# Opening with an fp32 spread of c's first row, and weight casts ordered behind a latent norm's squares

## The chip, the cores and the metric

The kernel runs on one core of one Trainium2 chip. A core has five engines with a queue each: PE (TensorE, the matmuls), DVE (VectorE), ACT (ScalarE), POOL (GpSimd) and SP (SyncE, which here only starts DMAs). Each executes its own list of instructions in order; semaphores make one list wait for another. The metric is the device time of one execution in microseconds (us).

## The reference

A two-layer hybrid transformer on 256 latent tokens and 256 context tokens of width 1024. Layer 0 mixes with grouped-query attention, layer 1 with a bidirectional mLSTM; each layer has a half feed-forward before and after its mixer, and everything is modulated by vectors made from `c` (latent) and `c_ctx` (context). Only the latent tokens come out. Cut to what the change touches:

```python
def half_ffn(h, shift, scale, gate, w_in, w_out, g, b):
    xm = modulate(h, shift, scale)
    a, u = jnp.split(xm @ w_in, 2, axis=-1)
    y = (jax.nn.silu(a) * u) @ w_out
    return post_norm(h, 0.5 * gate * y, g, b)          # layer norm of ALPHA*h + delta

for i in range(DEPTH):
    mod_lat = jnp.split((silu(c) @ ada_w[i] + ada_b[i])[:, None, :], N_MOD, axis=-1)
    mod_ctx = jnp.split((silu(c_ctx) @ ada_w[i] + ada_b[i])[None, None, :], N_MOD, axis=-1)
    h_lat = half_ffn(h_lat, mod_lat[0], mod_lat[1], mod_lat[2], ...)
    h_ctx = half_ffn(h_ctx, mod_ctx[0], mod_ctx[1], mod_ctx[2], ...)
    ...                                                 # mixer, post_norm, second half_ffn
return h_lat
```

## The kernel before

**Layout and precision.** Activations lie transposed: `h[:, d, t]` holds feature block d (eight blocks of 128) for 512 tokens, latents first. A product of full fp32 accuracy is made from three one-pass matmuls (`mm3`, L230, L233, L234): a tensor x is split into a rounded part `xh` and the rest `xl`, a weight chunk into `wh` and `wl`, and wh·xh + wh·xl + wl·xh is summed in PSUM. Plain fp32 matmuls, which the hardware makes in several passes, are left for small things.

**Weights.** A chunk of 128 x 1024 fp32 (512 KB) comes by DMA into a ring of `RAW = 4` buffers. `split` (L213 on ACT, L218 on DVE) makes `wh` by a cast on ACT and `wl` by subtractions on DVE, in four pieces of 256 columns in the feed-forwards, into a ring of `WB = 7` pairs. So a raw buffer is free for the next DMA only after the chunk's last low piece on DVE. Each of `split`'s instructions goes through `behind`: where `self.fence` names an instruction of the same engine, the new one is ordered behind it. This edge has no semaphore; it only constrains the order in which the scheduler writes out each engine's list at build time.

**The norms.** `norm` (n0 to n4, one behind each half feed-forward or mixer but the last) is a generator that `steps` advances between matmuls. For one group (latents `LAT` or context `CTX`) it does: the mean by a matmul with a constant (L425, as all its matmuls); per feature block d, z = h − mean on DVE (L447) and its square on ACT (L454); sums of the squares on DVE (L464) and POOL; the variance by 128x1 matmuls (L425); 1/sqrt in small steps (L483 to L486 and L271 to L275); a diagonal matrix of it on DVE (L490), spread over the partitions by another L425 matmul (`rb`); per block x, `xh`, `xl` (L520 on DVE, L521 on ACT, L522 on DVE), which the next weights' matmuls need. The latent norm comes first, the context norm some 10 to 20 us behind it. PE fills the waits with products of the weights that come next: rows of these products are placed between the norm's matmuls by the scheduler. n4 has a latent norm only and is "raw": `xh` and `xl` are made from z before the variance is known (L451, L452), so the first three units of the last feed-forward multiply un-normed data and are corrected behind it; their matmuls are 258 columns wide.

**The opening.** `start` makes the first modulation vectors itself. The 16 values of silu(c) per partition (`b.ct`, one set for the latents, v = 0, one for the context, v = 1) are spread by `replicate(v)` into rows that are equal on all partitions (`b.cb`), for dot products on DVE (`by_dve`). `by_pe(d)` makes the modulation of block d by 128x2 fp32 matmuls instead. `products(d)` then are the first feed-forward's matmuls, 512 columns wide. `b.ct` is split into `parts` (L1557, L1547), and `unit` is a copy of the identity in the one-pass type (L1556). All of it is pinned: its order is the order in which it is written.

Of the kernel before, what the change touches and what calls it, by code (L numbers as in the profile page):

```python
# [13 lines left out]
AF = mybir.ActivationFunctionType  # L14
# [4 lines left out]
P = 128  # L19
D = 1024  # L20
ND = D // P
# [138 lines left out]
class Body:  # L160
# [24 lines left out]
    def mm(self):  # L185
        return self.t([P, 512], tag="mm", bufs=6, pool=self.pp)
# [217 lines left out]
    def pin(self, ins):  # L404

        return self.tc.keep_in_program_order(ins)
# [14 lines left out]
    def norm(self, g, coef, keep=True, nxt=True, alone=False, log=False):  # L421


        nc, V, S = self.nc, self.nc.vector, self.nc.scalar
        mm = lambda *k, **kw: self.pin(nc.tensor.matmul(*k, **kw))  # L425
# [6 lines left out]
        v = 0 if t0 == 0 else 1  # L432
        most = g == LAT
# [10 lines left out]
        for d in range(ND):  # L444
            yield
            z = self.h[:, d, t0:t1]
            V.tensor_tensor(out=z, in0=z, in1=m[:, :w], op=ALU.subtract)  # L447
            if raw:
                c = coef()[1][:, v, d : d + 1]
                xh = self.xh[:, d, TL:T]  # L450
                S.activation(xh, z, AF.Copy, scale=c)  # L451
                V.scalar_tensor_tensor(self.xl[:, d, TL:T], z, c, xh.bitcast(F32), ALU.mult, ALU.subtract)  # L452
            q = self.tmp(w)
            S.activation(q, z, AF.Square)  # L454
            if d in (SQA if alone else SQPE):
                sums[d] = q, q
                continue
            eng = nc.gpsimd if d in (POOLA if alone else POOLD) else V
            if eng not in sums:
                sums[eng] = q, None  # L460
            else:
                a, s2 = sums[eng]
                s2 = s2 or self.t([P, TL], tag="s1", bufs=S1B)
                eng.tensor_tensor(out=s2, in0=a, in1=q, op=ALU.add)  # L464
                sums[eng] = s2, s2
# [10 lines left out]
        pin = self.pin  # L476
        if most:
# [3 lines left out]
            for i in range(n):  # L481
                c = var[:, n + i : n + i + 1]
# [11 lines left out]
        if most:  # L494
# [3 lines left out]
            for d in range(ND):  # L498
                if eng[d] is not V:
                    z = self.h[:, d, t0:t1]  # L500
# [10 lines left out]
        for d in range(ND):  # L511
            yield
            z = self.h[:, d, t0:t1]
            if most and eng[d] is V:
                V.tensor_tensor(out=z, in0=z, in1=dls, op=ALU.subtract)
            ab, c, e = coef()
# [57 lines left out]
    def ffn(self, layer, s, gate, groups, side, start=None):  # L574
# [7 lines left out]
        with self.tc.tile_pool(name=f"ffn{li}", bufs=1) as gp:  # L582
# [3 lines left out]
            if start:  # L586
                start(self)
                done = NSTART
# [892 lines left out]
def start(b):  # L1481

    nc, pin = b.nc, b.pin
    V, S = nc.vector, nc.scalar
    mm = lambda *k, **kw: pin(nc.tensor.matmul(*k, **kw))  # L1487
    dma = lambda *k: pin(nc.sync.dma_start(*k))
    rep = [[b.mm() for _ in range(2)] for _ in range(2)]
    acc = [b.mm() for _ in range(6)] + [b.ps()]  # L1490
    dots = b.ps()
    c0, e0, mod = b.modv(), b.modv(), b.t([P, 2, 2, ND])
    raws, ws = {}, {}

    def load_dots(d, chs=(1, 0)):
        if d not in raws:
            raws[d] = b.pair(F32)
        for ch in chs:
            dma(raws[d][ch], b.a["ada_p"][PEDOT.index((ch, d))] if (ch, d) in PEDOT else b.a["ada_w"][0, ch * ND + d])

    def load(d):
        dma(b.h[:, d, :], b.a["xt"][:, d, :])
        r = b.t([P, 1024], tag="raw", bufs=RAW)[:, : 7 * P]
        dma(r, b.a["start_in"][d][:, : 7 * P])
        ws[d] = [r] + b.pair(n=7 * P)
        pin(S.copy(ws[d][1], ws[d][0]))

    def bias(ch, d):
        return b.b1[:, d : d + 1] if ch else b.vec[:, V_ADAB + d : V_ADAB + d + 1]

    def replicate(v):
        for k in range(ND):
            for i, c in enumerate(parts):
                mm(rep[v][k // 4][:, k % 4 * P : (k % 4 + 1) * P], c[:, k, v : v + 1].broadcast_to([P, P]), unit, start=i == 0, stop=i == 1)
        for i in range(2):
            pin(V.tensor_copy(b.cb[:, v, i * 512 : (i + 1) * 512], rep[v][i]))

    def by_pe(d):
        o = {ch: dots[:, 4 * d + 2 * ch : 4 * d + 2 * ch + 2] for ch in (1, 0) if (ch, d) in PEDOT}
        for ch in o:  # L1520
            for k in range(ND):
                mm(o[ch], raws[d][ch][:, k * P : (k + 1) * P], b.ct[:, k, :], start=k == 0, stop=k == ND - 1)
        for ch in o:
            pin(S.activation((e0, c0)[ch][:, :, d], o[ch], AF.Identity, bias=bias(ch, d)))

    def by_dve(d):
        for ch in (0, 1):
            if (ch, d) not in PEDOT:
                for v in range(2):
                    to = mod[:, ch, v, d : d + 1]  # L1530
                    pin(V.scalar_tensor_tensor(b.tmp().bitcast(BF16), raws[d][ch], 1.0, b.cb[:, v, :], ALU.mult, ALU.mult, accum_out=to))
                pin(V.tensor_scalar((e0, c0)[ch][:, :, d], mod[:, ch, :, d], bias(ch, d), None, ALU.add))
                yield

    def modulated(d):
        xs = []
        for v, g in enumerate((LAT, CTX)):
            xs.append((b.xl[:, d, g[0] : g[1]], b.tmp(TL), b.xh[:, d, g[0] : g[1]]))
            b.later.append((b.h[:, d, g[0] : g[1]], ALPHA, None, None))
        for o in (2, 1):  # L1540
            for v, g in enumerate((LAT, CTX)):
                last = pin(S.activation(xs[v][o], b.h[:, d, g[0] : g[1]], AF.Identity, bias=e0[:, v, d : d + 1], scale=c0[:, v, d : d + 1]))
        b.fence = {last.ins.engine: last} if d == ND - 1 else {}
        return xs

    def low(l, x, h):
        return pin(V.tensor_tensor(out=l, in0=x, in1=h.bitcast(F32), op=ALU.subtract))  # L1547

    def products(d):
        for i, (w, x) in enumerate(((1, 0), (2, 0), (1, 1))):  # L1550
            for n, o in enumerate(acc):
                mm(o, ws[d][w][:, n * P : (n + 1) * P], b.x(d, BOTH)[x], start=not d and not i, stop=d == ND - 1 and i == 2)

    parts = [b.tmp(2 * ND).bitcast(F32R).rearrange("p (n f) -> p n f", f=2) for _ in range(2)]
    unit = b.tmp(P).bitcast(F32R)
    pin(V.tensor_copy(unit, b.ident))  # L1556
    pin(S.copy(parts[0], b.ct))  # L1557
    low(parts[1], b.ct, parts[0])
    replicate(0)
    load_dots(0)  # L1560
    load(0)
    replicate(1)
    low(ws[0][2], ws[0][0], ws[0][1])
    by_pe(0)
    load_dots(1)
    xs = {0: modulated(0)}
    for d in range(ND):
        n = d + 1
        rows = by_dve(n) if n < ND else iter(())
        if n < ND:  # L1570
            load(n)
        if n + 1 < ND:
            load_dots(n + 1)
        next(rows, None)
        for x in xs[d]:
            last = low(*x)
        for _ in rows:
            pass
        if n < ND:
            low(ws[n][2], ws[n][0], ws[n][1])  # L1580
            by_pe(n)
            xs[n] = modulated(n)
        products(d)
    b.fence[last.ins.engine] = last
    for j in range(NSTART - 1):
        b.ffn_g(j, acc[2 * j], acc[2 * j + 1], BOTH)
    r, (h, l) = b.t([P, 1024], tag="raw", bufs=RAW), b.pair()
    nc.sync.dma_start(r.rearrange("p (d f) -> p d f", d=ND), b.a["start_in"].rearrange("d p f -> p d f")[:, :, 7 * P :])
    b.split(r, h, l)
    o = b.mm()  # L1590
    for k in range(ND):
        c = slice(k * P, (k + 1) * P)
        b.mm3(o, (h[:, c], l[:, c]), b.x(k, BOTH), k == 0, k == ND - 1)
    b.ffn_g(NSTART - 1, acc[6], o, BOTH)


def emit(ctx, tc, a, out):
# [56 lines left out]
    both = (LAT, CTX)  # L1654
    feeds = [feed(q, dots, 0 if i else ROOM[0][1]) for i, (q, dots) in enumerate(zip(queue, DOTS))]
    norm("n0", lambda: b.ln_mod(0, 0, (0, 3)))
    b.ffn(0, 0, once("g0", lambda: b.half_gate(0, 2)), both, feeds[0], start)
    feeds[0].done()
    cpool.close()
    norm("n1", lambda: b.ln_mod(0, 1, (0, 6)), log={LAT: "kept", CTX: "kept"})  # L1660
    b.attention(lambda: b.shift_(0, 5))
    cpool = b.silu_c()
    b.pending = [lambda: b.silu_load(lambda ins: b.after(ins, b.silu) if ins.ins.engine == b.silu.ins.engine else ins)]
    norm("n2", lambda: b.ln_mod(0, 2, (1, 0)))
    b.ffn(0, 1, once("g1", lambda: b.half_gate(0, 8)), both, feeds[1])
    feeds[1].done()
# [106 lines left out]
```

## Time and profile before

| | us |
|---|---|
| median of three runs (lowest, highest) | 1653.3 (1652.46, 1655.67) |
| the profiled execution: its own time | 1652.55 |
| its span (first to last instruction) | 1650.6 |
| PE busy in it | 1617.8 (98%) |
| DVE busy | 1407.3 (85%) |
| ACT busy | 752.0 (46%) |
| POOL busy | 161.2 (10%) |

PE is busy nearly throughout, so the time is PE's work plus the few places where it waits. The largest of these waits is at the very start (6.36 us), the others, below 2.1 us each, are mostly in the norms. Busy shares of the other engines are averages: in a norm DVE is busy without a break. A matmul record is longer than its share of the pipeline (0.28 us for one of 256 columns that starts 0.12 us after the one before), so the work of a stretch is read from counts and starts, not from record lengths.

### The profile page before, as it was taken

To read this page: it belongs to the slowest core of one execution; us is meant where nothing else is said; L and a number is where in the kernel's file an instruction comes from. 1 tells how busy PE (TensorE), PEld (TensorE's weight loads), DVE (VectorE), ACT (ScalarE), POOL (GpSimd) and SP (SyncE) were. 2 spreads that over 40 slices of the span, in tenths; PEclk is the share of its full clock that TensorE was granted. 3 is DMA by queue.
4 is the path that set the end of the run, shared out by engine and by line. 5 is a ranking of instruction groups with operands and counts; after the bars stand their busy time and mean duration, and the time that the engine had idled before them with its cause. 6 is when DMAs were issued, how large, how long until landed. Compare 5 with 4: busy or idle time off the path is not lost. (4 is left out here: it accounts for less than half of the span.)

```text
span 1650.6 us, 27339 instructions
## 1 busy us (share of the span) xinstructions
PE 1617.8 (98%) x10496; PEld 1472.2 (89%) x10496; DVE 1407.3 (85%) x2859; ACT 752.0 (46%) x1370; POOL 161.2 (10%) x237
## 2 busy tenths in 40 slices
PE   8999999999999999999999999999999999999998
PEld 7888888889988998899899998998999978999986
DVE  5999999979888998888797899898797968997686
ACT  4632223315666364255354453453453646566542
POOL 0011111102231210000000200000001002120000
PEclk9999999999999999999999999999999999999999
DMA  6777777742202544435334444335232342437552
GB/s 257 269 255 253 228 248 240 233 153 87 65 1 63 182 151 142 153 123 162 111 116 141 179 153 141 115 111 184 90 121 98 96 141 77 134 105 260 180 179 75
DMA packets 72210, 250.65 MB, mean 152 GB/s; under 512 B 7952, under 2 KB 11024, under 8 KB 72080
## 3 DMA queue, kind: packets, MB, share of 16 engines
q1 hardware_dynamic: 53360, 182.93, 33.7%
q0 software_dynamic: 17856, 65.02, 12.3%
q8 instruction: 82, 1.34, 0.3%
q10 hardware_dynamic: 864, 0.96, 0.2%
q14 instruction: 48, 0.39, 0.1%
HBM read 247.83 MB, written 1.05 MB: 151 GB/s over the span
## 5 line engine op out<-in xcount | busy, mean ns | idle before, releaser
L233 PE MATMUL t<-t,t 128*128 128x256 f32 (+2 forms) x2072 | 676.2, 327 | 1.2 <-DVE t L522 0.8
L230 PE MATMUL t<-t,t 128*128 128x256 f32 (+2 forms) x2072 | 675.3, 328 | 1.8 <-ACT t L213 1.7
L234 PE MATMUL t<-t,t 128*128 128x256 f32 (+2 forms) x2072 | 673.3, 326 | 1.4 <-DVE t L218 1.4
L213 ACT CAST t<-t 128x1024 fp32r<-128x1024 f32 (+3 forms) x390 | 329.2, 866 | 308.9 <-PE t L234 145.7
L218 DVE TENSOR_TENSOR t<-t,t 128x256 fp32r<-128x256 f32 (+2 forms) x726 | 415.6, 613 | 50.0 <-ACT t L213 48.3
L233 PEld LDWEIGHTS t<-t,t 128*128 128x128 f32 x2072 | 391.2, 189 | 37.1 <-DVE t L522 1.5
L230 PEld LDWEIGHTS t<-t,t 128*128 128x128 f32 x2072 | 388.6, 189 | 38.3 <-ACT t L213 3.2
L234 PEld LDWEIGHTS t<-t,t 128*128 128x128 f32 x2072 | 389.6, 188 | 35.8 <-DVE t L218 1.6
L825 PEld LDWEIGHTS t<-t,t 128*128 128x128 f32 x2436 | 288.9, 189 | 3.2 <-ACT t L833 1.5
L825 PE MATMUL t<-t,t 128*128 128x256 f32 x2436 | 289.9, 281 | 1.4 <-ACT t L833 0.9
L338 DVE SCALAR_TENSOR_TENSOR t<-t,t 128x1024 bf16<-128x1024 f32 x224 | 265.8, 1218 | 1.6 <-DMA t<-in_ada_w 1.5
L760 ACT CAST t<-t 128x512 fp32r<-128x512 f32 (+1 forms) x116 | 108.7, 941 | 148.9 <-DVE t L762 103.7
L330 POOL DMA_DIRECT2D t<-in_ada_w x124 | 66.5, 536 | 798.2 <-DVE t L338 733.7
L761 DVE TENSOR_TENSOR t<-t,t 128x512 fp32r<-128x512 f32 (+1 forms) x116 | 125.3, 1086 | 6.8 <-ACT t L760 6.2
L624 DVE SCALAR_TENSOR_TENSOR t<-t,t,t 128x256 f32<-128x256 f32 x128 | 56.6, 477 | 49.6 <-PE t L234 49.6
L1033 PE MATMUL t<-t,t 128*128 128x256 f32 (+1 forms) x256 | 78.7, 308 | 1.0 <-DVE t L218 1.0
L1032 PE MATMUL t<-t,t 128*128 128x256 f32 (+1 forms) x256 | 79.2, 310 | 0.0
L1034 PE MATMUL t<-t,t 128*128 128x256 f32 (+1 forms) x256 | 78.7, 309 | 0.0
L568 ACT ACTIVATE t<-t 128x256 f32<-128x256 f32 (+1 forms) x64 | 30.1, 479 | 103.3 <-PE t L234 100.9
L1487 PE MATMUL t<-t,t 128*128 128x512 f32 (+2 forms) x280 | 61.1, 378 | 6.9 <-DVE t L1547 6.4
L1487 PEld LDWEIGHTS t<-t,t 128*128 128x128 f32 x280 | 53.5, 234 | 14.0 <-issue 6.3
L967 PE MATMUL t<-t,t 128*128 128x512 f32 x264 | 60.0, 389 | 0.0
(200 smaller groups left out, 1481.5 us busy)
## 6 DMA issues: line engine op xcount, KB each, us to landing
t<-in_ffn_in SPq DMA_DIRECT2D x168, 512.0 KB, 4.5
t<-in_ada_w POOLq DMA_DIRECT2D x124, 512.0 KB, 4.1
t<-in_ffn_out SPq DMA_DIRECT2D x68, 512.0 KB, 4.5
t<-in_ffn_last SPq DMA_DIRECT2D x22, 512.0 KB, 3.5
t<-in_ada_w SPq DMA_DIRECT2D x15, 512.0 KB, 8.5
t<-in_att_in SPq DMA_DIRECT2D x12, 512.0 KB, 3.8
t<-in_att_out SPq DMA_DIRECT2D x8, 512.0 KB, 3.6
t<-in_ml_qk SPq DMA_DIRECT2D x8, 512.0 KB, 3.6
```

Source lines behind the costliest of these rows:

```text
L213: self.behind(self.nc.scalar.copy(h, x))
L218: self.behind(self.nc.vector.tensor_tensor(out=ls, in0=xs, in1=hs.bitcast(F32), op=ALU.subtract))
L230: ins = mm(out, wh, xh, start=first, stop=False)
L233: mm(out, wh, xl, start=False, stop=False)
L234: mm(out, wl, xh, start=False, stop=last)
L338: ins = nc.vector.scalar_tensor_tensor(self.tmp().bitcast(BF16), r, 1.0, self.cb[:, v, :], ALU.mult, ALU.mult, accum_out=to)
L760: high = lambda p, r: pin(S.copy(p[0], r))
L761: low = lambda p, r: pin(V.tensor_tensor(out=p[1], in0=r, in1=p[0].bitcast(F32), op=ALU.subtract))
L825: pin(nc.tensor.matmul(o, p, q, start=first and k == i == 0, stop=k == half - 1 and i == 2, skip_group_check=True))
L1032: mm(o, self.xh[:, k, c], wh, start=k == 0, stop=False)
L1033: mm(o, self.xh[:, k, c], wl, start=False, stop=False)
L1487: mm = lambda *k, **kw: pin(nc.tensor.matmul(*k, **kw))
```

## The change

Two edits that do not touch each other.

```diff
@@ norm
-            S.activation(q, z, AF.Square)
+            square = S.activation(q, z, AF.Square)
+            if most and d == ND - 1:
+                self.fence = {square.ins.engine: square}
@@ start
-    def replicate(v):
+    def replicate(v, parts, unit):
         for k in range(ND):
             for i, c in enumerate(parts):
-                mm(rep[v][k // 4][...], c[:, k, v : v + 1].broadcast_to([P, P]), unit, start=i == 0, stop=i == 1)
+                mm(rep[v][k // 4][...], c[:, k, v : v + 1].broadcast_to([P, P]), unit, start=i == 0, stop=i == len(parts) - 1)
@@ start, the order
+    replicate(0, [b.ct], b.ident)
     parts = [...]
     unit = b.tmp(P).bitcast(F32R)
-    pin(V.tensor_copy(unit, b.ident))
     pin(S.copy(parts[0], b.ct))
     low(parts[1], b.ct, parts[0])
-    replicate(0)
+    pin(V.tensor_copy(unit, b.ident))
     load_dots(0)
     load(0)
-    replicate(1)
+    by_pe(0)
     low(ws[0][2], ws[0][0], ws[0][1])
-    by_pe(0)
+    replicate(1, parts, unit)
```

The opening: row v = 0 is spread by eight fp32 matmuls of `b.ct` itself with the identity, which need neither `parts` nor `unit`; row v = 1 still by sixteen one-pass matmuls, but behind `by_pe(0)`. The fence: in each latent norm (`most` is true for the latents), the square of the last block becomes ACT's fence, so every cast that `split` emits later in the program (weights, and the gated products of the feed-forward) is ordered behind it.

Lines 455 to 1519 of before are 2 higher in the change, later ones 5 higher; the names of the tiles that stand for one weight chunk are 8 lower. Three places of the engines' lists:

PE, the opening, before. `t_101` and `t_102` are the two `parts`, `t_103` is `unit`; `t_86` to `t_89` are the four halves of the two spread rows, `t_97` the dots of `by_pe(0)` (16 matmuls) and `by_pe(1)` (8), `t_90` the first product. The last two one-pass matmuls of the spread and what follows:

```order
L1487 MATMUL t_89<-t_103,t_101 128x128
L1487 MATMUL t_89<-t_103,t_102 128x128
L1487 MATMUL t_97<-t_72,t_125 128x2 x16
L1487 MATMUL t_97<-t_72,t_170 128x2 x8
L1487 MATMUL t_90<-t_68,t_131 128x512
```

And PE's first rows of the change (`t_72` is `b.ct`, `t_70` the identity):

```order
L1489 MATMUL t_86<-t_70,t_72 128x128 x4
L1489 MATMUL t_87<-t_70,t_72 128x128 x4
L1489 MATMUL t_97<-t_72,t_117 128x2 x16
L1489 MATMUL t_88<-t_113,t_111 128x128
L1489 MATMUL t_88<-t_113,t_112 128x128
```

32 one-pass matmuls ahead of `by_pe(0)` became 8 fp32 ones; 16 one-pass ones stand behind it now, ahead of `by_pe(1)`. Nothing else changes in PE's list up to the products.

PE, norm n1 (behind the attention), at the variance of its context norm (L425 into `t_5767`), before. The first chunks of the next feed-forward are `t_5711`, `t_5743`, `t_5800`, `t_5832`, `t_5873`:

```order
L234 MATMUL t_5869<-t_68,t_5873 128x256
L230 MATMUL t_5870<-t_68,t_5873 128x256
L233 MATMUL t_5870<-t_69,t_5873 128x256
L234 MATMUL t_5870<-t_68,t_5873 128x256
L230 MATMUL t_5869<-t_68,t_5873 128x256
L425 MATMUL t_5767<-t_61,t_5673 128x1
```

In the change the same place (the chunks are `t_5703`, `t_5735`, `t_5792`, `t_5824`, `t_5865` now, the variance `t_5759`):

```order
L230 MATMUL t_5699<-t_68,t_5735 128x256
L233 MATMUL t_5699<-t_69,t_5735 128x256
L230 MATMUL t_5700<-t_68,t_5735 128x256
L233 MATMUL t_5700<-t_69,t_5735 128x256
L234 MATMUL t_5699<-t_68,t_5735 128x256
L234 MATMUL t_5700<-t_68,t_5735 128x256
L425 MATMUL t_5759<-t_61,t_5665 128x1
```

Before, the 96 matmuls of the first four chunks and 13 of the fifth stand between PE's first use of the first chunk and this variance; in the change the 48 of the first two chunks and 8 others do. The 53 others stand behind the variance and ahead of the context's `rb` (82 matmuls between the two now, 29 before); from there on the two lists have the same rows again. On ACT the casts of the first four chunks moved behind the eight squares of n1's latent norm (three of them stood ahead of all squares, one between the sixth and the seventh), on DVE their low pieces accordingly.

ACT, norm n4, before: `t_15502` to `t_15705` are the first six chunks of the last feed-forward (two to a unit), `t_15395` the last chunk of the mixer's output; then the norm's blocks begin (`t_68` is `xh`):

```order
L213 CAST t_15395<-t_15393 128x1024
L213 CAST t_15502<-t_15500 128x1024
L213 CAST t_15534<-t_15532 128x1024
L213 CAST t_15601<-t_15599 128x1024
L213 CAST t_15633<-t_15631 128x1024
L213 CAST t_15673<-t_15671 128x1024
L213 CAST t_15705<-t_15703 128x1024
L451 ACTIVATE t_68<-t_67,t_15415 128x256
L454 ACTIVATE t_15432<-t_67 128x256
```

And in the change, from the last block's pair on:

```order
L451 ACTIVATE t_68<-t_67,t_15407 128x256
L454 ACTIVATE t_15482<-t_67 128x256
L213 CAST t_15494<-t_15492 128x1024
L213 CAST t_15526<-t_15524 128x1024
L213 CAST t_15593<-t_15591 128x1024
L213 CAST t_15625<-t_15623 128x1024
L213 CAST t_15665<-t_15663 128x1024
L213 CAST t_15697<-t_15695 128x1024
```

All six casts went from ahead of the sixteen block instructions to behind them, and two more casts that stood further on follow directly (before, one of these was between the sixth and seventh block). On DVE 22 of their low pieces went from ahead of the norm's blocks to between the blocks and the variance's L483, so that 23 pieces stand there. PE's list still has the 48 matmuls of the first two chunks ahead of the variance (54 of the first three before), and 14 matmuls of the mixer's last output between the mean and those.

In n0, n2 and n3 the shifts are smaller: one cast each moves from between two of the latent squares to behind the last, some later ones by a few rows, and PE's rows ahead of a norm's matmul change by at most 9.

More of the change, by code (lines that the diff above doesn't have):

```diff
@@ L1509, in bias @@
         return b.b1[:, d : d + 1] if ch else b.vec[:, V_ADAB + d : V_ADAB + d + 1]
-    def replicate(v):
+    def replicate(v, parts, unit):
         for k in range(ND):
             for i, c in enumerate(parts):
-                mm(rep[v][k // 4][:, k % 4 * P : (k % 4 + 1) * P], c[:, k, v : v + 1].broadcast_to([P, P]), unit, start=i == 0, stop=i == 1)
+                mm(
+                    rep[v][k // 4][:, k % 4 * P : (k % 4 + 1) * P], c[:, k, v : v + 1].broadcast_to([P, P]), unit,
+                    start=i == 0, stop=i == len(parts) - 1,
+                )
         for i in range(2):
```

## The prediction

> **What bounds the kernel now.** First the page's busy times, then the list of PE's waits (engine and line waited for, total, times, longest).
>
> ```profile
> PE 1617.8 (98%) x10496; PEld 1472.2 (89%) x10496; DVE 1407.3 (85%) x2859; ACT 752.0 (46%) x1370; POOL 161.2 (10%) x237
> ...
> PE t L1487 <- DVE t L1547: 6.4, 1, 6.4
> PE t L425 <- DVE t L464: 3.4, 3, 2.1
> PE t L425 <- DVE t L402: 3.2, 4, 1.3
> PE t L230 <- ACT t L213: 1.7, 3, 0.9
> PE t L234 <- DVE t L218: 1.4, 1, 1.4
> ```
>
> PE bounds the kernel. A change gains only by ending one of these waits and loses by making PE wait elsewhere. The largest wait is the start; the norms' waits (L425 behind sums and residuals on DVE) add up to some 6.6 us; PE waits for weight casts 1.7 us in all. So tying the casts back has little to gain, and the question is whether PE still has its weights in time. I take the opening first, then the norms where the order of PE's rows shifts most: n1 and n4.
>
> **The opening.** The timeline (start, duration, engine, line, operation, what ended the idle time) and a table by stretch (length; busy time and count of PE, PEld, DVE, ACT, POOL; granted clock, DMA share, GB/s):
>
> ```profile
> 2.94 0.22 ACT L316 ACTIVATE t<-t 128x16 f32<-128x16 f32 x1
> 5.91 0.17 DVE L319 TENSOR_SCALAR t<-t 128x8 f32<-128x8 f32 x1 [4.94 <-DMA t<-in_vec]
> 6.36 13.78 PE L1487 MATMUL t<-t,t 128*128 128x128 f32 x64 [6.36 <-DVE t L1547]
> 20.65 7.54 PE L1487 MATMUL t<-t,t 128*128 128x2 f32 x25 [0.51 <-ACT t L1524]
> ...
> 6.36:13.22 6.86, 6.86 (x33) 6.86 (x33) 2.08 (x3) 0.94 (x1) 0.00 (x0) 1.00 1.01 395
> 13.22:20.10 6.88, 6.88 (x33) 6.84 (x33) 4.21 (x7) 0.00 (x0) 0.00 (x0) 1.00 1.03 416
> 20.65:24.09 3.44, 3.44 (x17) 3.44 (x17) 0.85 (x2) 3.44 (x7) 0.00 (x0) 1.00 0.12 44
> 24.09:27.96 3.87, 3.87 (x10) 3.10 (x11) 3.75 (x7) 3.72 (x9) 0.00 (x0) 1.00 0.65 223
> 27.96:31.37 3.41, 3.41 (x16) 2.81 (x16) 3.37 (x8) 0.41 (x2) 0.00 (x0) 1.00 0.72 266
> ```
>
> PE starts at 6.36 only because `unit` and `parts` wait on DVE behind L319, which waits for a DMA. silu(c) itself is there at 2.94 + 0.22 = 3.16. Then come 32 one-pass matmuls (6.86, 0.21 each), `by_pe(0)` (16 matmuls in two records each, 6.88, so 0.43 a matmul), a wait of 0.51, `by_pe(1)` (3.44), and the products at 24.09.
>
> Now: start 3.2; eight fp32 matmuls of 128 columns, which the trace doesn't show. Nearest rows: the fp32 ones of 128x2 at 0.43, and L425's of 128x256 below, two records in 0.59. I take 0.43, the row of this place (bounds 0.43 and 0.59, so up to 1.3 us more): 3.4, to 6.6. `by_pe(0)` 6.9, to 13.5; 16 one-pass ones 3.4, to 16.9; `by_pe(1)` 3.4, to **20.3**. Its 0.51 wait goes, since L1524 runs beside the second spread. So the products start 3.8 earlier. DVE copies row 1 at 16.9 instead of 13.46 and does `by_dve(1)` (2.4 us, 15.06 to 17.47 before) later; that stands in the 4.6 us for which DVE idled before 22.25, and its first result for PE is wanted only by the third pass of the products.
>
> The products run at half pace at first: 10 in 3.87 us, then 16 in 3.41, although the granted clock reads 1.00 in both rows. The step at 27.96 ends the first stretch of 3.41 us that is full of 512-column products. Windows of that length that keep their phase would put the step at 24.55 now, 4.25 us behind the products' start instead of 3.87; that returns 0.2. **Opening: −3.6**, bounds −5.3 and −2.0 (phase, price).
>
> The Trainium skill, "TensorE: Matmul & The Clock Gate", Part 1, says that PE runs at half rate until one busy window of about 3.4 us and at full rate behind it. PE was busy from 6.36 to 20.1 here without reaching full pace, so the rule as it stands disagrees with this trace; by it, products would be at full pace from the first, and the opening's gain would be 3.8 instead of 3.6.
>
> **Norm n1.** PE's list has 53 products fewer ahead of the context's variance (L425) than before, so their time is lost unless the variance comes earlier. Does it? DVE alone in the stretches, then all engines in the last one, and the wait at the variance:
>
> ```profile
> 544.50:561.30 16.80, 12.82 (x36) 1.00 0.83 317
> 561.30:576.70 15.40, 15.29 (x42) 1.00 0.01 1
> 576.70:582.10 5.40, 5.39 (x14) 1.00 0.34 97
> ...
> 567.35:582.15 14.80, 13.74 (x112) 13.18 (x112) 14.68 (x38) 7.21 (x17) 2.58 (x4) 1.00 0.13 37
> 582.15 1.05 PE L425 MATMUL t<-t,t 128*128 128x1 f32 x8 [0.53 <-DVE t L464]
> 586.45 0.59 PE L425 MATMUL t<-t,t 128*128 128x256 f32 x2
> ```
>
> From 561.3 to the variance DVE never rests: it sets the variance's time. In this stretch its list holds the same amount of work as before: the 12 low pieces that left the front (544 to 547) are not done by then, 11 of them now stand behind the variance. The 4.0 us that they free lie ahead of 561, where DVE idled 16.80 − 12.82 = 4.0 us already, waiting for PE. So the variance stays near 582.15, and PE, with 14.80 us for 57 rows instead of 110, idles for 53 x 13.74/112 = 53 x 0.12 = 6.4 us more. Behind the variance 82 products instead of 29 stand ahead of `rb`; their low pieces come faster (0.34 us for six to twelve matmuls of 0.12) than PE uses them. So `rb` goes from 586.45 to about 592.9. **n1: +6.4**; it is 2.4 if DVE does come 4.0 earlier, 8.1 if the clock halves behind the gaps (below).
>
> **Norm n4.** ACT's casts and block instructions, PE's and DVE's rows around the mean, the variance and `rb`, and what a low piece costs (five in 1.76):
>
> ```profile
> 1441.46 1.76 DVE L218 TENSOR_TENSOR t<-t,t 128x256 fp32r<-128x256 f32 x5
> 1449.61 0.70 PE L425 MATMUL t<-t,t 128*128 128x256 f32 x2 [0.39 <-DVE t L402]
> 1450.80 0.51 ACT L451 ACTIVATE t<-t,t 128x256 fp32r<-128x256 f32 x1 [1.58 <-DVE t L447]
> 1455.40 1.03 ACT L213 CAST t<-t 128x1024 fp32r<-128x1024 f32 x1
> 1457.72 0.40 ACT L454 ACTIVATE t<-t 128x256 f32<-128x256 f32 x1
> 1459.58 1.72 PE L425 MATMUL t<-t,t 128*128 128x1 f32 x13
> 1461.01 0.35 DVE L483 TENSOR_SCALAR t<-t 128x1 f32<-128x1 f32 x2 [1.06 <-PE t L425]
> 1464.22 0.59 PE L425 MATMUL t<-t,t 128*128 128x256 f32 x2
> 1472.63 0.28 PE L230 MATMUL t<-t,t 128*128 128x256 f32 x1
> ...
> t<-in_ffn_in SPq DMA_DIRECT2D x11, 512.0 KB, 4.0
> ```
>
> The last square ends at 1458.12; without the cast at 1455.40 at about 1457.2. Only then the first of the six casts runs, to 1458.2, and its first low piece, to 1458.6. PE has 14 products behind the mean (1449.6 + 0.7 + 14 x 0.12 = 1452.0) and then needs that chunk: it idles some 6 us. 48 products (5.8) end at 1464.4, so the variance is 4.8 late. On DVE 23 low pieces of 0.34 (7.8) from 1458.2 stand ahead of L483: 1466.0, 5.0 late; to `rb` it took 3.2 before and has two pieces more (0.7): 1469.9. PE's own way, 30 products instead of 24 from the variance to `rb`, gives 1464.4 + 4.64 + 0.7 = 1469.7. The sixth chunk's DMA waits for the raw buffer of the first (ring of four and a spare), free at 1459.6; plus 4.0 and a cast that is 1464.6, in time for its pieces. `rb` is 5.6 late, then the same 66 products follow. **n4: +5.6** (4.0 if the blocks go faster; 9 with a later DMA or a slow clock).
>
> **n0, n2, n3.** One cast goes from among the latent squares to behind them, which ends them 1 us earlier, and three more low pieces (1.0) stand ahead of the latent L490; by the context's mean 0.7 of it is left, partly made up. I take 0.2 each, and in n3 0.5 more, since nine products (1.1) went from ahead of the context's `rb` to behind it. **+1.1**, bounds 0 and 3.3. The largest norm wait, in n2, stays, with the slow stretch behind it:
>
> ```profile
> L213 ACT CAST t<-t 128x1024 fp32r<-128x1024 f32 x1 | 1.0, 1048 | 1.3 <-DMA t<-in_ffn_in 1.3
> ...
> 932.50:935.90 3.40, 1.34 (x12) 1.13 (x11) 2.37 (x4) 1.31 (x5) 2.50 (x4) 1.00 0.99 349
> 935.90:939.32 3.42, 3.42 (x17) 3.42 (x18) 2.12 (x7) 0.00 (x0) 0.00 (x0) 0.50 1.01 392
> ```
>
> A cast among the context's squares waits 1.3 us for its DMA; an earlier chunk takes its place in the list, but that chunk's buffer is freed by a low piece at the very place of DVE's list that freed the other's, so it waits alike.
>
> **Sum**, against the profiled execution's 1652.55 us: −3.6 + 6.4 + 5.6 + 1.1 = +9.5, so **1662.0**. The median of the runs is 0.75 above that execution, the spread of the runs larger; I leave it.
>
> **Rivals.** (1) DVE has room after all at n1: if its context rows move up by the 4.0 us of freed pieces, n1 costs 2.4 and the time is 1658. Against it: the 4.0 us of idle time ahead of 561. (2) The clock: in n2 2.06 us of idle time in one window halved the next (17 matmuls in 3.42 us, clock 0.50), which cost 1.7. n4's 6 us surely do so once, n1's gaps may, since PE would be busy under half of the time. Each full slow window that meets work costs 1.7; three make 1667. In n4 part of it hides behind DVE's 7.8 us. The same section of the Trainium skill wants an idle window of about 3.4 us for this; by that n1's gaps cost nothing, but 2.06 us sufficed here. (3) **Not slower**: eight dense fp32 matmuls might open the clock in the opening, where the one-pass ones did not. From then on the 13.7 us of small matmuls could take half, −6.9, and the products' slow start goes, another −2: 1653. It decides at the first `by_pe`: 0.2 instead of 0.43 a matmul. Against it: one window of dense work is all that there is, and then 128x2 ones follow. It is what the Trainium skill's rule, Part 1 above, would say of dense work; the trace shows only that 13.7 us of thin matmuls did not do it.
>
> **How the numbers follow.** Forecast 0.64, (1) 0.14, (2) 0.12, (3) 0.06, something unseen that makes it faster 0.04. The forecast's own range is 1659 to 1665; with (1), (2) and the bounds of the terms, the range is 1654 to 1668. A measurement of this kernel tells about 0.2% (3.3 us) from no change: faster 0.04, same 0.10 ((3) and the low end of (1)), slower 0.86.
>
> **What would show it.** Products at 20.3 and PE's first wait 3.2; in n1 about 8 us of waits for L522's results between the latent `rb` and the context's variance, which stays 14.8 us behind the first chunk's first product; in n4 one wait of PE for an ACT cast of 6 us, and L483 late behind L218 pieces. The forecast is wrong if n1's context variance comes within 12 us of that first product, or if PE's wait in n4 is below 4 us.

## The result, and the profile after

The change is slower by half a per cent: 1662.83 us (median of six executions, 1660.98 to 1666.35) against 1654.93 for the kernel before on the same chip (six, 1652.46 to 1657.7), ratio **1.0050 [1.0034, 1.0065]**. The same kernel was measured twice more for the experiments below, with 1.0068 [1.005, 1.0085] and 1.0098 [1.0082, 1.0114]. So it loses 8 to 17 us, and how much differs from one measurement to the next. The forecast was 1662.0 with a range of 1654 to 1668. Its sign held; that its number met the first median is partly luck, as the terms show.

The page after (busy times), then the list of PE's waits (engine and line waited for, total, times, longest):

```profile
PE 1619.1 (98%) x10496; PEld 1471.7 (89%) x10496; DVE 1408.6 (85%) x2859; ACT 751.3 (45%) x1370; POOL 159.7 (10%) x237
...
PE t L230 <- ACT t L213: 8.8, 4, 7.1
PE t L234 <- DVE t L218: 5.3, 5, 2.6
PE t L1489 <- ACT t L316: 3.2, 1, 3.2
PE t L425 <- DVE t L402: 2.5, 3, 1.0
PE t L233 <- DVE t L524: 2.3, 3, 1.3
```

The opening's wait fell from 6.4 to 3.2. In its place PE waits for weights: for casts on ACT (L213) 8.8 instead of 1.7, for low pieces on DVE (L218) 5.3 instead of 1.4, which is what a fence must show if it makes the casts come too late. The wait for the squares' sums (L425 behind L464 on DVE, 3.4 before) has left the list; at those places PE now waits for weights instead. Counts of instructions are those of before.

**The bill by terms.** PE's records stand in the same order in both kernels outside the norms, so the start of the k-th record after, less that of the k-th before, tells how far the kernel is ahead or behind. The median of this difference is taken over a calm stretch ahead of and behind each norm; the steps between are what each part cost. Three profiles of the same kernel (the two others are of runs e5 and e10):

| term | forecast | first profile | e5 | e10 |
|---|---|---|---|---|
| opening | −3.6 | −7.3 | −3.4 | −3.3 |
| n0 | +0.2 | −0.2 | −0.3 | +0.1 |
| n1 | +6.4 | +7.2 | +8.5 | +8.5 |
| n2 | +0.2 | −2.5 | −2.0 | +2.6 |
| n3 | +0.7 | +2.2 | +2.4 | +2.3 |
| n4 | +5.6 | +9.2 | +9.8 | +8.1 |
| end of PE's list | +9.5 | +8.5 | +14.9 | +18.3 |

The signs of the large terms are right. n1, n3 and n4 were priced too low, by 6 to 8 us together, and in the first profile the opening and n2 gave 6.4 more than priced. (Of e5's 9.8 for n4, 0.9 comes behind the norm, around 1500 us, where it also comes in e1 and e6, which have no fence in n4.)

**The opening.** The table by stretch, from PE's start to the first dozen products, in the first profile after (columns as in the prediction's tables: length; busy time and count of PE, PEld, DVE, ACT, POOL; granted clock, DMA share, GB/s):

```profile
3.21:6.63 3.42, 3.42 (x18) 3.42 (x18) 0.76 (x2) 0.18 (x1) 0.00 (x0) 1.00 1.01 389
6.63:9.94 3.31, 3.31 (x33) 3.31 (x31) 0.91 (x3) 0.94 (x1) 0.00 (x0) 0.98 0.98 380
9.94:17.19 7.25, 7.25 (x35) 7.25 (x36) 4.88 (x8) 3.94 (x10) 0.00 (x0) 0.50 1.03 416
17.19:20.90 3.71, 3.71 (x12) 2.95 (x12) 3.71 (x7) 3.50 (x8) 0.00 (x0) 0.62 1.03 412
```

And the same places in e5, the same kernel:

```profile
3.21:6.86 3.65, 3.65 (x17) 3.65 (x18) 0.76 (x2) 0.19 (x1) 0.00 (x0) 1.00 0.99 373
6.86:13.73 6.87, 6.87 (x35) 6.87 (x34) 2.00 (x4) 1.02 (x2) 0.00 (x0) 1.00 1.01 405
13.73:20.30 6.57, 6.57 (x32) 6.57 (x33) 3.79 (x7) 3.85 (x9) 0.00 (x0) 1.00 1.03 416
20.30:24.29 3.99, 3.99 (x11) 3.12 (x12) 3.99 (x8) 3.78 (x8) 0.00 (x0) 1.00 0.80 287
```

In both PE starts at 3.21, behind the wait for L316 in the list above, and the eight fp32 matmuls take 3.4 to 3.6 (priced at 3.4). In e5 everything up to the products follows with 0.21 from one record's start to the next, and the products start at 20.30, as forecast. In the first profile the 33 records from 6.63 to 9.94 take 0.10 each: the clock was open for one stretch, from 6.39 to 9.80 by its own record, then it reads 0.50 and the pace is 0.21 again. The products start at 17.19. (The reading of 1.00 in rows of half pace, as at 3.21 to 6.63 and throughout e5's opening, says only that no change was recorded yet: the trace's first one is at 6.39 here and at 24.98 in e5. The spacing of the records decides.)

**n1.** The timeline's rows of PE that waited, from the first product of the next feed-forward to the context's variance, after:

```profile
561.56 0.74 PE L230 MATMUL t<-t,t 128*128 128x256 f32 x4 [1.64 <-ACT t L523]
562.76 0.58 PE L233 MATMUL t<-t,t 128*128 128x256 f32 x1 [0.46 <-DVE t L524]
569.34 0.70 PE L425 MATMUL t<-t,t 128*128 128x256 f32 x2 [1.02 <-DVE t L402]
573.97 0.50 PE L234 MATMUL t<-t,t 128*128 128x256 f32 x2 [2.55 <-DVE t L218]
```

And the table by stretch, from that product to the variance, from there to `rb`, and a part of the latter:

```profile
561.56:575.52 13.96, 9.70 (x59) 8.80 (x59) 13.84 (x35) 7.07 (x17) 2.71 (x4) 0.88 0.01 1
575.52:587.71 12.19, 12.19 (x93) 12.19 (x92) 10.89 (x35) 6.94 (x14) 0.00 (x0) 0.86 0.69 216
576.80:579.57 2.77, 2.77 (x14) 2.77 (x14) 2.77 (x11) 2.70 (x5) 0.00 (x0) 0.50 0.60 179
```

From the first product to the context's variance (575.52) DVE is busy 13.84 of 13.96 us and PE 9.70; before it was 14.68 and 13.74 of 14.80. So the variance is DVE's, and came 0.8 earlier behind the first product, not 4.0. The waits sum to 5.7 here, not the forecast's 8, and only 2.1 of it is for the norm's own results (L523, L524, which the forecast calls L522's); the longest, 2.55, is for a low piece. PE waits less than forecast because its 59 records took 9.70, 0.16 each, at a clock of 0.88 on average; while DVE sets the time this costs nothing. Behind the variance 12.19 us pass to `rb` instead of 4.30, for 82 products instead of 29. At 0.12 each the 53 more are 6.4; most of the other 1.5 is in the 14 records at half clock from 576.80 to 579.57, which at 0.12 each would take 1.7 instead of 2.77.

**n4.** PE's rows at the mean, the wait, the variance and `rb`, after:

```profile
1448.41 0.70 PE L425 MATMUL t<-t,t 128*128 128x256 f32 x2
...
1457.85 0.58 PE L230 MATMUL t<-t,t 128*128 128x258 f32 x1 [7.10 <-ACT t L213]
1466.41 1.94 PE L425 MATMUL t<-t,t 128*128 128x1 f32 x14
1471.82 0.59 PE L425 MATMUL t<-t,t 128*128 128x256 f32 x2
```

The stretch from the end of the wait to the variance:

```profile
1457.85:1466.41 8.56, 8.56 (x49) 8.56 (x50) 7.78 (x23) 5.83 (x6) 0.00 (x0) 0.65 0.67 204
```

PE waits 7.10 us for the first cast (the forecast had "some 6"), and then needs 8.56 for the 48 products that were priced at 5.8: the clock reads 0.65. ACT's rows and then DVE's around it:

```profile
1456.05 0.51 ACT L451 ACTIVATE t<-t,t 128x256 fp32r<-128x256 f32 x1 [0.92 <-DVE t L447]
1456.46 0.40 ACT L454 ACTIVATE t<-t 128x256 f32<-128x256 f32 x1
1456.77 4.82 ACT L213 CAST t<-t 128x1024 fp32r<-128x1024 f32 x5
...
1457.83 7.80 DVE L218 TENSOR_TENSOR t<-t,t 128x256 fp32r<-128x256 f32 x23 [0.75 <-ACT t L213]
1467.84 0.35 DVE L485 TENSOR_SCALAR t<-t 128x1 f32<-128x1 f32 x2 [2.21 <-PE t L425]
```

ACT waited 0.92 for the last block's z (L447 on DVE), so DVE paced the end of the blocks. The chain is the forecast's: last square, cast, 23 low pieces in 7.80. But then DVE idles 2.21 for PE's variance (L485 is L483 of before): PE at half clock ends last here, not the pieces.

### The profile page after: what moved, and what is told of

It reads as the page before. It is cut to its first block, busy times and chain, and to the rows that moved or that the text cites. A ratio compares the mean times of both kernels' runs of the same rounds, so it can differ in the third digit from the quotient of the medians.

```text
span 1659.0 us, 27324 instructions
## 1 busy us (share of the span) xinstructions
PE 1619.1 (98%) x10496; PEld 1471.7 (89%) x10496; DVE 1408.6 (85%) x2859; ACT 751.3 (45%) x1370; POOL 159.7 (10%) x237
## 5 line engine op out<-in xcount | busy, mean ns | idle before, releaser
L230 PE MATMUL t<-t,t 128*128 128x256 f32 (+2 forms) x2072 | 678.8, 329 | 10.7 <-ACT t L213 8.8
L213 ACT CAST t<-t 128x1024 fp32r<-128x1024 f32 (+2 forms) x390 | 329.0, 866 | 303.5 <-PE t L234 122.1
L218 DVE TENSOR_TENSOR t<-t,t 128x256 fp32r<-128x256 f32 (+2 forms) x726 | 414.5, 613 | 46.5 <-ACT t L213 43.9
L230 PEld LDWEIGHTS t<-t,t 128*128 128x128 f32 x2072 | 391.4, 189 | 47.5 <-ACT t L213 10.5
L234 PEld LDWEIGHTS t<-t,t 128*128 128x128 f32 x2072 | 391.0, 189 | 41.3 <-DVE t L218 6.8
L233 PEld LDWEIGHTS t<-t,t 128*128 128x128 f32 x2072 | 392.9, 190 | 37.6 <-DVE t L524 3.4
L827 PEld LDWEIGHTS t<-t,t 128*128 128x128 f32 x2436 | 288.6, 189 | 3.6 <-ACT t L835 1.5
L454 ACT ACTIVATE t<-t 128x256 f32<-128x256 f32 x72 | 26.2, 412 | 82.8 <-DVE t L447 82.8
L1489 PE MATMUL t<-t,t 128*128 128x512 f32 (+2 forms) x280 | 57.4, 365 | 3.2 <-ACT t L316 3.2
```

Of the source, the lines that this page charges most:

```text
L213: self.behind(self.nc.scalar.copy(h, x))
L218: self.behind(self.nc.vector.tensor_tensor(out=ls, in0=xs, in1=hs.bitcast(F32), op=ALU.subtract))
L230: ins = mm(out, wh, xh, start=first, stop=False)
L233: mm(out, wh, xl, start=False, stop=False)
L234: mm(out, wl, xh, start=False, stop=last)
L827: pin(nc.tensor.matmul(o, p, q, start=first and k == i == 0, stop=k == half - 1 and i == 2, skip_group_check=True))
```

## Experiments

The theory: the two edits are independent and add up; the opening gains what its start and its open stretch give, and the fence loses nearly everything in n1 and n4, where PE runs out of products. Rivals: the opening's gain is lost behind it; the loss comes from the fence elsewhere; the open clock comes from the new order, not from fp32; the half clock behind the waits has another cause than idling.

**e1 and e2: one edit each.** e1 is before with the opening's part of the diff, e2 is before with the `norm` part.

> The opening of the change alone; no fence in the norms. Theory A (the opening saves 7.3 us, since PE starts at 3.2, has 24 small matmuls fewer and runs by_pe(0) at full pace behind the dense fp32 matmuls; all that the change loses is the fence): products start at about 17.2, PE's list at every norm is as before, and the time is 7.3 us below before, 1647.5, ratio 0.9955; up to 1.7 less if the slow window behind n2's 2.06 us wait falls elsewhere. Rival B (the clock's part of it, some 3.3 us, is given back at the next wait for a DMA or for DVE): 3.8 us below before, ratio 0.9977.

> The fence alone; the opening as before. Theory A: the difference of the whole change (+8) less the opening's -7.3: +15 us, ratio 1.009, of it some 7 at n1 and some 9 at n4, with PE's wait for an ACT cast of about 7 us in n4. Rival C (the two edits meet: the fence hurts only because the earlier opening shifts the clock's windows or the DMAs): below +10 us, ratio under 1.006.

e1: 1644.71 (1643.21 to 1647.4), ratio **0.9957 [0.9944, 0.9971]**, so −7.3 against 1651.98 for before, measured beside it. e2: 1670.88 (1670.06 to 1671.51), **1.0118 [1.0092, 1.0143]**, +18.9. The opening alone is a clear gain that nothing behind it takes back, and the fence alone a clear loss. Their sum, +11.6, lies between the first and the last measurement of the whole.

**e3 and e4: the whole, without the fence in one norm.** (`raw` is true in n4 alone; `log` has this value in n1 alone.)

```diff
-            if most and d == ND - 1:
+            if most and d == ND - 1 and not raw:            # e3
+            if most and d == ND - 1 and log != "kept":      # e4
```

> The whole change, but no fence in n4. Theory A: n4 costs what the trace shows there, 9.5 us, so 9.5 below the change: 1 to 2 us below before, ratio 0.999. Prediction's own price of n4: 5.6 below the change, ratio 1.0015. Rival C: n4's list being free, other stalls fill in; within 3 us of the change.

> The whole change, but no fence in n1, so PE's list around n1 has the 53 products back ahead of the context's variance. Theory A: n1's 8.5 us less the 1.4 that came back by 608: 7.1 below the change, 1 us above before, ratio 1.0005. Rival D (DVE and the clock set n1, the list doesn't): within 2 us of the change, ratio 1.004.

e3: 1658.37 (1654.96 to 1666.51), 1.005 [1.0029, 1.0071]; e4: 1659.43 (1654.63 to 1665.83), 1.0049 [1.0032, 1.0067]. By the medians neither gives back what its norm was expected to, and the executions spread over 11 us. The profiles are plainer. In e3, n4 costs +0.2 and n1 still +7.5; in e4, n1 costs −0.5 and n4 +10.7. What hides it is n2, which costs +2.1 and +4.8 in these two profiles.

**e6: fence in n0, n2 and n3 alone**, with the new opening; **e5** is the change itself, beside it.

> The whole change once more, on the chip and in the rounds of the next three, so that they can be compared with it. By the earlier two parts (opening -7.3, fence +18.9) it is 11.6 us above before; by its own first measurement 7.9. In its profile: a wait of 7.1 us for an ACT cast in n4, and at n2 a wait of 0.3 to 4.6 us, by how the weight DMA there meets the DMAs that POOL starts.

> The whole change, but no fence in n1 and in n4. Theory A (n1 and n4 cost some 7 and 9.5 us, as the difference of the two traces has it, and e3 and e4 did not show it in full because n2's wait is a matter of luck in each execution): 14 to 17 us below the whole change, so 2 to 6 below before, ratio 0.996 to 0.999, and 2 to 5 above the opening alone. Rival E (what leaves n1 and n4 comes back at n2 and n3, since the fence's lists there go with it): within 8 us of the whole change, ratio 1.000 or more.

e5: 1666.19 (1662.15 to 1670.15), 1.0068 [1.005, 1.0085]. e6: 1649.89 (1645.25 to 1656.8), 0.9984 [0.997, 0.9999]. Taking the fence from n1 and n4 together is worth **16.3 us**, close to what the profiles give for the two terms (8.5 + 9.8 in e5, less the 0.8 that e6 keeps there: 17.5). In e6 PE's rows around n4's mean, variance and `rb` stand as before:

```profile
1445.21 0.70 PE L425 MATMUL t<-t,t 128*128 128x256 f32 x2 [0.38 <-DVE t L402]
1454.61 0.39 PE L233 MATMUL t<-t,t 128*128 128x258 f32 x1 [0.30 <-DVE t L452]
1455.20 1.93 PE L425 MATMUL t<-t,t 128*128 128x1 f32 x14
1459.87 0.60 PE L425 MATMUL t<-t,t 128*128 128x256 f32 x2
```

14.66 us from the mean to `rb`, 23.41 in the change. The fence in n3 keeps its price (+2.3 in e6's profile).

**e7 and e8: what opens the clock in the opening?** Both are without the fence. e7 spreads both rows by fp32 matmuls ahead of `by_pe(0)`; e8 has the change's order, but spreads both rows by one-pass matmuls. Against the change's opening:

```diff
@@ e7
+    replicate(0, [b.ct], b.ident)
+    replicate(1, [b.ct], b.ident)
...
-    replicate(1, parts, unit)
@@ e8
-    replicate(0, [b.ct], b.ident)
     pin(V.tensor_copy(unit, b.ident))
+    replicate(0, parts, unit)
```

> The opening alone, but both rows of c spread by fp32 matmuls at the very start, 16 in a row. Theory F (dense fp32 matmuls open the clock; in the change it was open from 6.6 to 10 us and closed again over thin ones): eight at 0.43, eight at 0.21, then by_pe(0) at 0.11 a record and part of by_pe(1) too; products at 13.5 to 15.5 instead of 17.2, time 2 to 4 us below the opening alone, unless DVE's vectors are late then. Rival G (by_pe(0) ran fast for another reason, such as the order): 16 at 0.43 are 6.8 us, products no earlier than 17, time within 0.5 us of the opening alone.

> The opening alone with the change's order (by_pe(0) ahead of row 1), but row 0 spread by sixteen one-pass matmuls as before. Theory F (the clock): PE starts at 6.3, by_pe(0) takes 6.9 us as before, products at 23.5, time 0.6 us below before, ratio 0.9996. Rival G (the order makes by_pe(0) fast): by_pe(0) in 3.5 us, products at 20.1, time 4 us below before, ratio 0.9976.

e7: 1645.74 (1645.04 to 1649.04), 0.9945 [0.9926, 0.9964]. e8: 1653.93 (1650.66 to 1656.36), **1.0 [0.9987, 1.0013]**. So the order gives nothing that the time shows (by the bill its opening is 1.1 ahead of before's); the gain is that of fp32. e8's opening is at half pace throughout: the 18 records of the one-pass spread and the 34 and 32 behind it all at 0.19 to 0.21:

```profile
6.39:9.77 3.38, 3.38 (x18) 3.38 (x18) 0.69 (x1) 0.41 (x1) 0.00 (x0) 1.00 1.03 381
9.77:16.63 6.86, 6.86 (x34) 6.86 (x34) 1.69 (x2) 0.60 (x2) 0.00 (x0) 1.00 1.02 413
16.63:23.20 6.57, 6.57 (x32) 6.57 (x33) 3.78 (x7) 3.86 (x9) 0.00 (x0) 1.00 0.70 283
```

e7 did not clearly gain more than e1, though it was expected to. Its profile has the open stretch too, from 8.16 us on, but again only one, and products at 17.86.

**e9 and e10: is the half clock in n4 a matter of PE's idling?** e9 is the change with ten matmuls in n4 that nothing reads; they come to stand exactly where PE waited. e10 is the change, for comparison.

```diff
                 self.fence = {square.ins.engine: square}
+                if raw:
+                    idle = self.ps()
+                    for _ in range(10):
+                        mm(idle[:, :w], self.mean, self.h[:, 0, t0:t1], start=True, stop=True)
```

> The change, with ten fp32 matmuls of 128x256 (0.59 us each, 5.9 in all) on PE in n4, behind the 14 products that follow the mean and ahead of the first weight cast's products; they add work that nothing reads, and stand where PE waited 7.1 us. Theory C (the half clock behind that wait is caused by PE's idling and costs 2.2 us): the wait is about 1.2, the 26 products at 0.21 us behind it are gone, PE is through the 48 products 2.7 us earlier, and rb follows 2.2 earlier, where DVE's 23 low pieces end (in the profile of the change DVE idled 2.21 between the last piece and the variance's steps); the time is about 2 us below the change's in this call. Rival D (the slow stretch has another cause, or the time is DVE's alone): the half pace stays or rb does not move; the time is that of the change or above.

> The change as it stands, for comparison on the same chip: ratio 1.005 to 1.007 as in the two measurements so far. Its profile tells once more whether the opening had its window at full pace: products at 17.2 (window) or 20.3 (none).

e9: 1665.82 (1663.22 to 1672.31), 1.0084 [1.0065, 1.0103]; e10: 1670.79 (1666.16 to 1672.92), 1.0098. The intervals overlap, and e9's profile had the open stretch in the opening and e10's had not, so the 5 us between them say nothing of n4. e10's 1.0098 also lies above the 1.005 to 1.007 that was expected of it. n4 by itself, e9 and then e10:

```profile
1453.40 0.70 PE L425 MATMUL t<-t,t 128*128 128x256 f32 x2
1455.59 4.48 PE L425 MATMUL t<-t,t 128*128 128x256 f32 x20
1462.85 0.39 PE L230 MATMUL t<-t,t 128*128 128x258 f32 x1 [2.79 <-ACT t L213]
1470.26 1.93 PE L425 MATMUL t<-t,t 128*128 128x1 f32 x14
1475.67 0.59 PE L425 MATMUL t<-t,t 128*128 128x256 f32 x2
...
1464.41:1467.63 3.22, 3.22 (x18) 3.22 (x16) 3.22 (x11) 2.18 (x3) 0.00 (x0) 0.50 0.63 195
```

```profile
1459.23 0.70 PE L425 MATMUL t<-t,t 128*128 128x256 f32 x2
1468.66 0.58 PE L230 MATMUL t<-t,t 128*128 128x258 f32 x1 [7.09 <-ACT t L213]
1476.21 1.94 PE L425 MATMUL t<-t,t 128*128 128x1 f32 x14
1481.62 0.59 PE L425 MATMUL t<-t,t 128*128 128x256 f32 x2
```

The test was too weak: the ten matmuls took 4.48 us, not 5.9, so PE still idled 2.79, and a stretch of half clock followed all the same (16 products at the half pace, as in e10). Neither theory is decided by it. What the profiles do give is a price. The change's three profiles have 26, 22 and 16 products of n4 at half pace, and mean to `rb` takes 23.41, 23.07 and 22.39 us, so each costs about 0.10. The stretch costs n4 at most what DVE idled ahead of L485 in them, 2.21, 1.88 and 1.19, since without it the low pieces would end last. A part of n1's 8 is of this kind too.

**e11 and e12: e1 and e7 again, on one chip.**

> The opening alone, beside the next one on the same chip. Theory F' (eight dense fp32 matmuls last 3.4 us, as long as one window of the clock, so they fill one only where the phase happens to fit): products at 17.2 or at 20.3, nothing between, and runs that spread over 3 us; 1645 to 1648. Rival G' (the window opens for another reason than density, or the two sessions differed by chip): always 17.2.

> Both rows spread by fp32 matmuls, 16 of them, 6.9 us dense: theory F' says that this always holds a full window, so products at 17.9 each time (17.86 in the first profile), and the median is equal to or up to 2 us below the opening's alone; runs closer together. Rival G': products at 20.3 sometimes too.

e11: 1644.72 (1643.82 to 1647.34), **0.9948 [0.9936, 0.996]**; e12: 1648.35 (1646.64 to 1651.5), 0.9972 [0.996, 0.9984]. The opening alone is the better one here, against the expectation; by the bill e11's opening gains 7.1 us (e1's 6.9) and e12's 5.8 (e7's 6.2). e12's stretches:

```profile
3.21:9.05 5.84, 5.84 (x27) 5.84 (x28) 1.77 (x4) 0.11 (x1) 0.00 (x0) 1.00 0.99 377
9.05:12.51 3.46, 3.46 (x34) 3.46 (x32) 3.06 (x4) 0.83 (x1) 0.00 (x0) 0.98 1.03 408
12.51:17.87 5.36, 4.85 (x24) 4.77 (x24) 2.48 (x7) 3.87 (x9) 0.00 (x0) 0.50 1.03 418
```

The open stretch came once more, towards the end of the dense fp32 matmuls, and lasted one stretch of 3.4 us. Over all profiles: 16 dense fp32 matmuls opened the clock in two of two, eight of them in six of nine (not in e5, e6 and e10), one-pass ones in none of three (before, e2, e8). With eight, the products start at 17.2 with it and at 20.3 without, nothing between.

## Why the prediction was right in sign and close by luck

**What bounds the kernel:** held. What the change gained is the opening's wait and pace, and what it lost are mainly new waits of PE for weights, products moved behind a wait, and the half clock behind these waits.

**Opening, −3.6.** The steps up to the products held: start, price of an fp32 matmul, products at 20.3 (e5, e6, e10: −3.3 to −3.4). The 0.2 for the products' pace did not come: its step stood at 24.98, 24.98 and 25.19 in them, not at 24.55, since each execution has a phase of its own. What failed is the step that gave the third rival 6 in 100: its mechanism does happen, but for one stretch. It decides where the rival said, about the first `by_pe`: 0.11 from record to record instead of 0.21. The rest of the rival, that everything up to the products stays fast, never happened. So the opening is −3.4 or −7.3, by execution.

**n1, +6.4.** The mechanism held: DVE sets the variance and comes only 0.8 earlier, not the freed 4.0 us (first rival out), so the 53 products that were moved cost their own time. The size was low by 0.8 to 2.1, for the half clock behind the gaps, which was the second rival's.

**n4, +5.6.** The mechanism held at first: casts behind the squares, PE idle until the first one, 23 pieces behind it. The wait was mis-sized, 7.10 and not about 6: the last square ended 8.4 us behind the mean's start (1448.41 to 1456.86), not 7.6 as reckoned. The forecast took the cast that left the blocks as time gained, but ACT then waited for DVE's z there. And one step of the path failed: the low pieces were to end last. 16 to 26 products ran at half pace, which the forecast let DVE's pieces hide; DVE was through 1.2 to 2.2 us earlier, so most of it was not hidden. That is the second rival's mechanism at its place, and with its weight of 12 in 100 too low; "three full slow windows, 1667" is nearer to the second and third measurement (1666.2, 1670.8) than the forecast is.

**n0, n2, n3, +1.1.** n0 and the small shifts held. n3 costs 2.1 to 2.6 in each of the seven profiles that have the fence there and can be set against before row by row, three times its 0.7 (at most 0.3 in four of the five without, and 1.6 in e7, with a stretch at half clock from 1288.16); its cause is open. For n2 a fixed price was the wrong idea. The wait in it follows a DMA, as these rows of ACT (the cast among the context's squares) and of PE (the longest wait behind it) show, from the change's first profile and from e4:

```profile
931.54 1.05 ACT L213 CAST t<-t 128x1024 fp32r<-128x1024 f32 x1 [1.23 <-DMA t<-in_ffn_in]
935.42 0.38 PE L234 MATMUL t<-t,t 128*128 128x256 f32 x1 [1.84 <-DVE t L218]
```

```profile
926.85 1.04 ACT L213 CAST t<-t 128x1024 fp32r<-128x1024 f32 x1 [3.95 <-DMA t<-in_ffn_in]
930.71 0.58 PE L234 MATMUL t<-t,t 128*128 128x256 f32 x1 [4.55 <-DVE t L218]
...
929.15:939.39 10.24, 8.68 (x40) 8.63 (x41) 7.52 (x23) 3.40 (x6) 1.71 (x3) 0.50 0.74 238
```

1.23 and 1.84 here, 3.95 and 4.55 there (in e2 0.86 and 0.35, in e10 2.39 and 2.81), with lists of n2 that are the same. Against before n2 is −2.9 to +4.8 in the seven profiles with the fence and +1.1 to +4.0 in the five without. The wait itself is the smaller part: it grows by 2.7 of the 7.3 us between these two profiles. The rest goes with the half clock behind it, which lasts 3.41 us in before, none in the first profile, e2, e5 and e6 (−2.9 to −2.0), 3.41 in e3 (+2.1), 6.83 in e1, e7, e10, e11 and e12 (+1.1 to +2.6) and 10.24 in e4 (last row above, +4.8) and e8 (+4.0). Why the transfer lands late in some executions is open. n2 accounts for much of the spread of e3 and e4, and with the opening's stretch for the 8 to 17 us that one kernel was measured to lose: between the first profile and e10's the opening makes 4.0, n2 5.1 of the 9.8.

**Sum.** n1, n3 and n4 came to 18.6 in the first profile, against 12.7 forecast; the opening and n2 gave back 6.4 more than priced. That the first median met the forecast is these two errors against each other. With the measured sizes the sum is about +12 (open stretch) or +16 (none), n2 aside.

## What to carry to other kernels

Work that fills another engine's waits must not be ordered behind the very chain that causes the wait: the casts that were tied back behind the norm's squares were what PE lived on meanwhile, and their work came back as idle time, plus a stretch at half clock behind each idle one. Where two edits touch different places, price and run them apart: here the opening alone is a gain of 0.4 to 0.5%, 1644.7 us in both measurements, that the fence hid. And a term that depends on a transfer or on the clock's phase has a spread, not a price; it belongs into the range.

## What the hardware showed that was not expected

PE's busy time alone does not open the clock. Eight fp32 matmuls of 128 columns opened it in six of nine executions and sixteen in two of two, but one-pass ones of the same shape, at the same 0.21 a record, in none of three, though before and e2 have 6.9 us of them. 128x2 fp32 matmuls behind it let it fall back after one stretch of 3.41 us.

The traces also show when eight suffice. In each profile all changes of the granted clock lie whole multiples of 3.41 us apart (6.39, 9.80, 20.04 and 562.76 in the change's first one), as if the clock were decided once per window of that length, with a phase that differs by execution. In the six executions that opened, one such window held 2.65 to 3.37 us of the eight matmuls; in the three that did not, the fullest held 2.07 to 2.29 (their windows are reckoned back from the step at 24.98 or 25.19). The Trainium skill, "TensorE: Matmul & The Clock Gate", Part 1, has a window of about 3.4 us that runs freely against the kernel's start; these traces agree, though no run here moved the phase on purpose.

Idling far below such a window halves the clock too. PE idled 2.06 us in one window in n2 of before, and 1.85 (of the wait of 2.79) in one in e9's n4, and the next window ran at half pace, with 17 and 18 records in it. Between the opening and PE's last matmul, every window at full clock in the 14 profiles in which PE idled 1.78 us or more, 23 in all, was followed by one at half pace; of 154 with 0.63 to 1.69 us of idling only 8 were, and of those with less, none. After the 7.1 us of idling in n4, 16, 22 or 26 products ran at half pace.
